# The decode tile and the first full tile of an input projection share each weight block: five products a block, x in halves, wide dummy products

## The chip, the cores and the metric

One core of a Trainium2 chip runs the whole layer in one launch. The metric is the device time of a run in microseconds (us); less is better. The kernel before took 2188.03 us (median of 3 runs, 2186.51 to 2188.49). TensorE (PE) multiplies matrices; VectorE (DVE), ScalarE (ACT) and GpSimd (POOL) work on elements; SyncE (SP) here only starts DMA transfers. ACT and POOL start some too.

## The reference

The layer steps 2048 frames of a new stream and 64 frames of a running one (the decode frames), each of 1024 values. What the change touches is its first line, the projection of the normed frames by one weight with 2816 columns:

```python
def _project(a, w_in, pos):
    z = a @ w_in                                   # a: frames x 1024, w_in: 1024 x 2816
    qa, ka, va, qr, kr, vr, gr = jnp.split(z, SPLITS, axis=-1)
    ...                                            # rotate qa, ka, qr, kr by position

a = _rmsnorm(hp, norm1[l])                         # hp: 2048 prompt frames
qa, ka, va, qr, kr, vr, gr = _project(a, w_in[l], pos_p)
attn_o = _swa_prompt(qa, ka, va, sinks[l])
ret_o, s_p = _retention_prompt(qr, kr, vr)
hp = hp + _mix_out(attn_o, ret_o, gr, w_out[l])
hp = hp + _sqrelu_mlp(_rmsnorm(hp, norm2[l]), w_up[l], w_down[l])
...                                                # the same for hs, the 64 decode frames
```

`_attend` is attention over a window with sinks, `_retention_chunk` a recurrent attention by chunks with a state. Everything is fp32, the keys, values and states are outputs as well, and the last norm ends the layer.

## The kernel before

**Tiles.** The frames form 17 tiles: 16 full ones of 128 prompt frames, and the decode tile of 64 frames, here S (its index in the code is `S`, 16). The columns of the weight are worked in two phases of 1408 (`ph`), each in three column groups `ci` of 384, 512 and 512 columns: group 0 has the attention's query, key and value, groups 1 and 2 the retention's. The first unit of phase 0 is the pair (S, tile 0). Tile 0 is the first full tile, T below; the tile after it is the third tile. The unit goes through the groups in the order S group 0, T group 0, S group 1, T group 1, S group 2, T group 2; the units after it have one tile each.

**Products.** An fp32 value is kept as a high part and a low part, and a product of two values is made of three: high times high, high times low, low times high. The 1024 rows of a weight group lie in 8 blocks `k` of 128 rows. For a full tile each block takes three products: xh with wh (L599), xh with wl (L600), xl with wh (L602). The decode tile has only 64 frames, so its high and low parts lie side by side in one operand xh of 128 columns, and two products do (L599, L600); then the two halves of the result are added (`zb` L607, `zz` L608). The result z of a group is gathered in one PSUM bank.

**Loads and splits.** A weight block comes by SP's queue (`load_w`, L117) into a raw buffer, and `split_scaled` makes wh on ACT (L85) and wl on DVE (L86), scaled by the norm's gain `gsb`. The raw blocks of group 0 and 1 have eight buffers between them. The transposed x of a tile comes by `load_x` (L140) or, for the first two tiles, in two halves of four blocks (`load_part`, L640). `split_x` makes xh on ACT (L151) and xl on DVE for the first two tiles (L153), on POOL in four pieces for all later ones (L156). xh and xl have two buffers each, so the third tile's xh goes into S's buffer, once S's last product is done. For a full tile, the halves and the whole x are read from `xt`, where the 128 values of one row, block and tile (512 bytes) lie together.

**Order.** At the program's start ACT issues S's first half of x, the gains and S's second half; SP issues the eight blocks of group 0 (0-weights: a "c-weight" is a block of group c), then T's two halves, then the 1-weights, S's rows of x for the norm (`xk`, by `load_aux`), the 2-weights with the cache `cf` (L482, L483), the states. ACT and DVE split S's x, the eight 0-weights, then T's x. Eighteen dummy products (`idle`, L634) go first on PE. PE and SP follow the order in which the code is written. ACT, DVE and POOL are ordered by a scheduler.

**Small stages.** Between the products of the groups a planner sets the short stages of attention and retention of each tile (att_a to att_e, ret_a to ret_e). `run_ready` is asked before each block; it goes by a modelled clock that each block's products move on, by latencies `LAT` and by costs `COST`, and sets a stage when its inputs are due. So a change in the order of the products changes where the stages of the tiles behind it stand. Names of the stages' instructions that come up: `zr` and `qk` are rotated by three instructions on DVE and one addition on POOL (L215); pq (L267 to L271) and ptr (L415) are transposes on PE; rqT (L425) and rkT (L423) are copies of ptr that pss (L431), a product of the retention stage, waits for. `token_norm` (L176 to L179) and `token_rest` (L187 to L189) make the norm's factors; nsk (L667) holds the negated sinks.

Of the kernel before, what the change touches and what calls it, by code (L numbers as in the profile page):

```python
# [11 lines left out]
F32 = mybir.dt.float32  # L12
F32R = mybir.dt.float32r
AF = mybir.ActivationFunctionType
# [25 lines left out]
def body(ctx, tc, xt, xd, xtok, w1, wout, wup, wdn, gains, sinks, ck, cv, sret, rot, rdec, qdec, dmask,  # L40
# [93 lines left out]
    def load_x(t, first=False, tag="xr"):  # L134
        t0, T = tok(t)
        xr = xp.tile([128, NK, 128], F32, name="xr", tag=tag, bufs=1)
        if T < 128:
            xr = xr.rearrange("p k t -> p (k t)")[:, :NK * T].rearrange("p (k t) -> p k t", k=NK)
        if not first:
            nc.sync.dma_start(xr, xt[:, :, t0:t0 + T] if T == 128 else xd)  # L140
        return xr

    def split_x(t, xr, first=False):

        t0, T = tok(t)
        xh = xp.tile([128, NK, 128], F32R, name="xh")
        xl = xp.tile([128, NK, 128], F32R, name="xl") if T == 128 else None
        for a in (slice(0, 4), slice(4, 8)) if first else (slice(0, 8),):
            h = xh[:, a, :T]
            l = xl[:, a, :] if T == 128 else xh[:, a, 64:128]  # L150
            nc.scalar.activation(h, xr[:, a, :T], AF.Copy)  # L151
            if first:
                nc.vector.tensor_sub(l, xr[:, a, :T], h.bitcast(F32))  # L153
            else:
                for k in range(0, NK, 2):
                    nc.gpsimd.tensor_sub(l[:, k:k + 2], xr[:, k:k + 2, :T], h[:, k:k + 2].bitcast(F32))  # L156
        return xh, xl
# [12 lines left out]
    last_act, last_dve = [None], [None]  # L170
# [415 lines left out]
    def group(ph, t, ci, n_):  # L586
# [7 lines left out]
        z = psum("z") if (n_, ci) == (1, 2) else zp.tile([128, 512], F32, name="z")  # L594
        for k in range(NK):
            run_ready(clock[0])
            s = ws[ph, ci][k]
            wh, wl = s[:, 0], s[:, 1]
            nc.tensor.matmul(z[:, :n], xh[:, k], wh, start=k == 0, stop=False)  # L599
            nc.tensor.matmul(z[:, :n], xh[:, k], wl, start=False, stop=k == NK - 1 and xl is None)  # L600
            if xl is not None:
                nc.tensor.matmul(z[:, :n], xl[:, k], wh, start=False, stop=k == NK - 1)  # L602
            clock[0] += (2 if xl is None else 3) * n * 0.4237e-3
# [13 lines left out]
        if (n_, ci) == (0, 1):  # L617
            do_stage("att_a", *tiles[1])
            done["z0", 1] = clock[0]

    slow = {0: 2.4, 1: 2.4, **dict.fromkeys((2, 4, 15, 16, 17, 18, 20, 32), 2.0)}
# [11 lines left out]
    for _ in range(18):  # L633
        nc.tensor.matmul(idle[:, 0:128], idr, ones, start=True, stop=True)  # L634
    a, b = tiles[:2]
    xraw = {0: load_x(a[1], True)}

    def load_part(n, k):
        t0, T = tok(tiles[n][1])
        (nc.sync if n else nc.scalar).dma_start(xraw[n][:, k:k + 4, :T], xt[:, k:k + 4, t0:t0 + T] if T == 128 else xd[:, k:k + 4])  # L640

    load_part(0, 0)
    nc.scalar.dma_start(gsb, gains)
    load_part(0, 4)
    first = cp.tile([128, 3], F32, name="first")
    nc.scalar.activation(first, mhalf, AF.Copy)
    raws = [load_w(0, 0, k, True) for k in range(NK)]
    x0 = split_x(a[1], xraw[0], True)
    ws[0, 0] = weights(0, 0, raws)
    xraw[1] = load_x(b[1], True, "xk")  # L650
    for k in range(2):
        load_part(1, 4 * k)
    x1 = split_x(b[1], xraw[1], True)
# [10 lines left out]
    raws.append(load_w(0, 2, NK - 1))  # L664
    load_states(0)
# [588 lines left out]
def _arrays(x_prompt, x_sample, cache_k, cache_v, state_ret, norm1, w_in, sinks, w_out, norm2, w_up, w_down, norm_f):  # L1254
# [22 lines left out]
    return dict(xt=xt, xd=f(xt[:, :, SEQ:]), xtok=f(xa), w1=w1, wout=wout, wup=wup, wdn=wdn,  # L1277
# [23 lines left out]
```

## Time and profile before

| | before |
|---|---|
| runs, median (3) | 2188.03 us (2186.51 to 2188.49) |
| the profiled execution's own time | 2188.54 us |
| its span in the profile | 2186.8 us |
| granted TensorE clock, mean over the span | 0.998 |
| PE busy | 2169.5 us, 99% of the span |
| weight loads of PE (PEld) busy | 2085.7 us, 95% |
| DVE, ACT, POOL busy | 70%, 52%, 20% |
| moved by DMA | 515.92 MB, 236 GB/s |

The profile is of one execution, whose own time is 1.74 us longer than its span; times in its rows count from the span's start. A row of the timeline gives the start of an instruction, its duration, engine, line and operation, output <- inputs, the shape, and in brackets how long the engine had waited and for what. Of a matmul the duration overlaps the next one's start, so the pace is read from one start to the next. A row of the groups has the busy time and the mean duration in ns, then the idle time ahead of the group and what ended most of it. A row of the DMA issues has the number of transfers, the size of one and the median time from issue to landing.

### The profile page before, as it was taken

How to read it: one execution, taken by the hardware profiler on the slowest of the kernel's cores; microseconds unless marked ns; L12 is line 12 of the kernel's file. 1: busy time of each engine (PE TensorE's matmuls, PEld its weight loads, DVE VectorE, ACT ScalarE, POOL GpSimd, SP SyncE). 2: the span in 40 equal slices, each digit the busy share in tenths (PEclk: the TensorE clock that was granted, in tenths of full speed). 3: DMA queues.
4: the chain of work that ended last, by engine and by line, in shares of the span. 5: the costliest groups of instructions: out<-in, count | busy, mean ns of one | idle time of the engine just before them, and what ended most of it. 6: DMA issues, size and time to landing. Idle time of an engine off the chain costs nothing.

```text
span 2186.8 us, 35871 instructions
## 1 busy us (share of the span) xinstructions
PE 2169.5 (99%) x13170; PEld 2085.7 (95%) x13170; DVE 1519.9 (70%) x2698; ACT 1139.6 (52%) x2114; POOL 439.5 (20%) x577
## 2 busy tenths in 40 slices
PE   9999999999999999999999999999999999999998
PEld 7888888889888999999999999999999999999998
DVE  6576668566666685887787677667666876687665
ACT  6455555544445533555665566556545544554452
POOL 4545554444433222000000000000001200120011
PEclk9999999999999999999999999999999999999999
DMA  6667964788544897699799678666977777777662
GB/s 193 182 180 197 246 180 132 198 220 214 136 118 144 314 328 243 218 313 313 254 350 323 229 265 293 235 231 218 375 251 240 275 269 239 245 277 272 231 214 82
DMA packets 242927, 515.92 MB, mean 236 GB/s; under 512 B 21168, under 2 KB 128368, under 8 KB 238656
## 3 DMA queue, kind: packets, MB, share of 16 engines
q1 hardware_dynamic: 232224, 469.35, 63.3%
q0 software_dynamic: 8512, 43.29, 9.3%
q8 instruction: 103, 1.69, 0.3%
q10 hardware_dynamic: 2016, 1.00, 0.2%
q14 instruction: 72, 0.59, 0.1%
HBM read 411.19 MB, written 169.54 MB: 266 GB/s over the span
## 4 chain that ended last, share of the span: by engine, by line
PE 90%; DVE 1%; DMA 1%; ACT 1%; issue 0%; POOL 0%; SPq 0%; DVEq 0%; ACTq 0%
PE y L1165 10%; PE y L1164 10%; PE y L1163 10%; PE z L599 6%; PE z L600 6%; PE z L602 6%; PE b L999 4%; PE b L998 4%; PE b L997 4%; PE y L857 3%; PE y L859 3%; PE y L858 3%; PE a L999 3%; PE a L998 3%; PE a L997 3%; PE c L999 3%
## 5 line engine op out<-in xcount | busy, mean ns | idle before, releaser
L1165 PE MATMUL y<-vh,wd 128*128 128x352 f32 x1344 | 434.0, 323 | 0.8 <-DVE wd L534 0.8
L1164 PE MATMUL y<-vl,wd 128*128 128x352 f32 x1344 | 433.5, 323 | 0.0
L1163 PE MATMUL y<-vh,wd 128*128 128x352 f32 x1344 | 431.4, 321 | 0.0
L599 PE MATMUL z<-w,xh 128*128 128x512 f32 (+1 forms) x816 | 320.3, 392 | 0.1
L1115 POOL TENSOR_TENSOR acc<-acc,sq 128x352 f32<-128x352 f32 x41 | 71.1, 1735 | 1213.3 <-ACT sq L1114 1213.3
L600 PE MATMUL z<-w,xh 128*128 128x512 f32 (+1 forms) x816 | 305.7, 375 | 1.2 <-DVE w L86 1.1
L533 ACT ACTIVATE wd<-dr 128x1024 fp32r<-128x1024 f32 x168 | 177.4, 1057 | 246.5 <-PE y L1165 175.3
L533 ACT ACTIVATE wu<-upr 128x512 fp32r<-128x512 f32 x336 | 209.3, 627 | 177.7 <-PE b L999 88.2
L602 PE MATMUL z<-w,xl 128*128 128x512 f32 (+1 forms) x768 | 287.0, 374 | 0.1
L534 DVE TENSOR_TENSOR wu<-upr,wu 128x512 fp32r<-128x512 f32 x336 | 230.5, 692 | 72.1 <-ACT wu L533 57.9
L534 DVE TENSOR_TENSOR wd<-dr,wd 128x1024 fp32r<-128x1024 f32 x168 | 209.0, 1246 | 97.3 <-ACT wd L533 96.6
L1165 PEld LDWEIGHTS y<-vh,wd 128*128 128x128 f32 x1344 | 252.7, 188 | 1.1 <-DVE wd L534 1.1
L1164 PEld LDWEIGHTS y<-vl,wd 128*128 128x128 f32 x1344 | 252.4, 188 | 0.0
L1163 PEld LDWEIGHTS y<-vh,wd 128*128 128x128 f32 x1344 | 252.3, 188 | 0.0
L998 PE MATMUL b<-al,wu 128*128 128x352 f32 x576 | 185.8, 323 | 0.0
L999 PE MATMUL b<-ah,wu 128*128 128x352 f32 x576 | 185.5, 323 | 0.0
L997 PE MATMUL b<-ah,wu 128*128 128x352 f32 x576 | 184.9, 321 | 0.0
L600 PEld LDWEIGHTS z<-w,xh 128*128 128x128 f32 x816 | 154.9, 190 | 19.8 <-DVE w L86 3.5
L599 PEld LDWEIGHTS z<-w,xh 128*128 128x128 f32 x816 | 154.8, 190 | 16.9 <-ACT w L85 0.4
L534 DVE TENSOR_TENSOR vl<-rv,vh 128x1408 fp32r<-128x1408 f32 x84 | 137.6, 1640 | 43.4 <-ACT vh L533 42.9
L602 PEld LDWEIGHTS z<-w,xl 128*128 128x128 f32 x768 | 144.1, 188 | 21.6 <-DVE xl L153 0.4
L533 ACT ACTIVATE vh<-rv 128x1408 fp32r<-128x1408 f32 x84 | 116.0, 1381 | 63.9 <-DMA rv<-vscr 46.4
(291 smaller groups left out, 4777.4 us busy)
## 6 DMA issues: line engine op xcount, KB each, us to landing
rv<-vscr SPq DMA_DIRECT2D x84, 704.0 KB, 5.4
vscr<-C SPq DMA_DIRECT2D x48, 1056.0 KB, 5.7
upr<-uscr SPq DMA_DIRECT2D x192, 256.0 KB, 5.1
dr<-sscr SPq DMA_DIRECT2D x96, 512.0 KB, 4.7
upr<-in_wup SPq DMA_DIRECT2D x144, 256.0 KB, 3.8
dr<-in_wdn SPq DMA_DIRECT2D x72, 512.0 KB, 5.4
uscr<-in_wup POOLq DMA_DIRECT2D x16, 1024.0 KB, 10.0
sscr<-in_wdn POOLq DMA_DIRECT2D x16, 1024.0 KB, 9.0
```

What stands on the lines that cost most here:

```text
L533: nc.scalar.activation(h, x, AF.Copy)
L534: return nc.vector.tensor_sub(l, x, h.bitcast(F32))
L599: nc.tensor.matmul(z[:, :n], xh[:, k], wh, start=k == 0, stop=False)
L600: nc.tensor.matmul(z[:, :n], xh[:, k], wl, start=False, stop=k == NK - 1 and xl is None)
L602: nc.tensor.matmul(z[:, :n], xl[:, k], wh, start=False, stop=k == NK - 1)
L997: nc.tensor.matmul(o, wh, ah[:, k], start=k == 0 and i in (1, 6, 5), stop=False, skip_group_check=True)
L998: nc.tensor.matmul(o, wh, al[:, k], start=False, stop=False, skip_group_check=True)
L999: nc.tensor.matmul(o, wl, ah[:, k], start=False, stop=k == 3 and i in (2, 4, 3), skip_group_check=True)
L1115: nc.gpsimd.tensor_add(self.acc, self.acc, sq)
L1163: nc.tensor.matmul(o, wh, vh, start=f == 0, stop=False)
L1164: nc.tensor.matmul(o, wh, vl, start=False, stop=False)
L1165: nc.tensor.matmul(o, wl, vh, start=False, stop=f == 15)
```

## The change

The first unit, S and T, is made in another way in phase 0; all else stays.

1. **Products.** For each block S's two products are followed by T's three. In group 0 T lags two blocks behind S. `group` makes the products of both when it is called for S; when it is called for T, it takes the z that is there. T's z of groups 1 and 2 is in the pool `pp`, that of group 0 in `zp`.
2. **x in halves.** A new input `xq` holds each full tile's x on its own, so that half a tile's row lies together (2048 bytes instead of four pieces of 512). T's first half is issued by ACT, its second by SP between the fifth and the sixth 0-weight. ACT's queue now issues the gains, S's first half, T's first half, S's second half. ACT and DVE split in this order: S's first half, 0-weights 0 and 1, T's first half, 0-weights 2 and 3, S's second half, 0-weight 4, T's second half, 0-weights 5 to 7.
3. **Dummies.** Nine of 512 columns in place of eighteen of 128.
4. **Third tile.** Its x is issued on SP right behind the last 2-weight, ahead of the states. T's attention stage att_a is bound to be issued behind the newest split of x on ACT.

```diff
 def load_x(t, first=False, tag="xr"):
-            nc.sync.dma_start(xr, xt[:, :, t0:t0 + T] if T == 128 else xd)
+            nc.sync.dma_start(xr, xq[t] if T == 128 else xd)
...
 def split_x(t, xr, first=False):
-        for a in (slice(0, 4), slice(4, 8)) if first else (slice(0, 8),):
+        def part(a):
...
-            nc.scalar.activation(h, xr[:, a, :T], AF.Copy)
+            last_xh[0] = nc.scalar.activation(h, xr[:, a, :T], AF.Copy)
...
+        if first:
+            return (xh, xl), part
+        part(slice(0, 8))
         return xh, xl
...
 def group(ph, t, ci, n_):
-        z = psum("z") if (n_, ci) == (1, 2) else zp.tile([128, 512], F32, name="z")
-        for k in range(NK):
-            run_ready(clock[0])
...
+        def products(z, x, k):
+            h, l = x
+            wh, wl = ws[ph, ci][k][:, 0], ws[ph, ci][k][:, 1]
+            nc.tensor.matmul(z[:, :n], h[:, k], wh, start=k == 0, stop=False)
+            nc.tensor.matmul(z[:, :n], h[:, k], wl, start=False, stop=k == NK - 1 and l is None)
+            if l is not None:
+                nc.tensor.matmul(z[:, :n], l[:, k], wh, start=False, stop=k == NK - 1)
+            clock[0] += (2 if l is None else 3) * n * 0.4237e-3
+
+        if n_ != 1:
+            z = zp.tile([128, 512], F32, name="z")
+            pair = [(z, xs[ph, t][:2], 0)]
+            if n_ == 0:
+                other[ci] = psum("z") if ci else zp.tile([128, 512], F32, name="z")
+                pair.append((other[ci], xs[tiles[1]][:2], 0 if ci else 2))
+            for k in range(NK + pair[-1][2]):
+                run_ready(clock[0])
+                for y, x, lag in pair:
+                    if 0 <= k - lag < NK:
+                        products(y, x, k - lag)
+        else:
+            z = other[ci]
...
         if (n_, ci) == (0, 1):
-            do_stage("att_a", *tiles[1])
+            with tc.issue_after(last_xh[0].ins):
+                do_stage("att_a", *tiles[1])
...
-    for _ in range(18):
-        nc.tensor.matmul(idle[:, 0:128], idr, ones, start=True, stop=True)
+    for _ in range(9):
+        nc.tensor.matmul(idle, idr, ones.unsqueeze(1).broadcast_to([128, 4, 128]), start=True, stop=True)
...
-    load_part(0, 0)
     nc.scalar.dma_start(gsb, gains)
-    load_part(0, 4)
+    load_part(nc.scalar, 0, 0)
+    load_part(nc.scalar, 1, 0)
+    load_part(nc.scalar, 0, 4)
...
-    raws = [load_w(0, 0, k, True) for k in range(NK)]
-    x0 = split_x(a[1], xraw[0], True)
-    ws[0, 0] = weights(0, 0, raws)
...
+    raws = [load_w(0, 0, k, True) for k in range(5)]
+    load_part(nc.sync, 1, 4)
+    raws += [load_w(0, 0, k, True) for k in range(5, NK)]
...
+    lo, hi = slice(0, 4), slice(4, 8)
+    for f, y, ks in ((part0, lo, (0, 1)), (part1, lo, (2, 3)), (part0, hi, (4,)), (part1, hi, (5, 6, 7))):
+        f(y)
+        ws[0, 0] += weights(0, 0, raws, ks)
...
     raws.append(load_w(0, 2, NK - 1))
+    xraw[2] = load_x(tiles[2][1])
     load_states(0)
```

PE's order at the start of the program, before the change: the dummies, then S's products of group 0 (z_293 is S's result, xh_149 its x, w1_0_0_k the 0-weight k). T's follow behind the sixteenth.

```order
L634 MATMUL idle_108<-ones_73,idr_71 128x128 x18
L599 MATMUL z_293<-w1_0_0_0_154,xh_149 128x384
L600 MATMUL z_293<-w1_0_0_0_154,xh_149 128x384
L599 MATMUL z_293<-w1_0_0_1_157,xh_149 128x384
L600 MATMUL z_293<-w1_0_0_1_157,xh_149 128x384
L599 MATMUL z_293<-w1_0_0_2_160,xh_149 128x384
L600 MATMUL z_293<-w1_0_0_2_160,xh_149 128x384
```

The same place now; z_286 and xh_143 are S's, z_287, xh_144 and xl_145 are T's, and the lines are those of the changed code.

```order
L652 MATMUL idle_108<-ones_73,idr_71 128x512 x9
L601 MATMUL z_286<-w1_0_0_0_148,xh_143 128x384
L602 MATMUL z_286<-w1_0_0_0_148,xh_143 128x384
L601 MATMUL z_286<-w1_0_0_1_151,xh_143 128x384
L602 MATMUL z_286<-w1_0_0_1_151,xh_143 128x384
L601 MATMUL z_286<-w1_0_0_2_156,xh_143 128x384
L602 MATMUL z_286<-w1_0_0_2_156,xh_143 128x384
L601 MATMUL z_287<-w1_0_0_0_148,xh_144 128x384
L602 MATMUL z_287<-w1_0_0_0_148,xh_144 128x384
L604 MATMUL z_287<-w1_0_0_0_148,xl_145 128x384
L601 MATMUL z_286<-w1_0_0_3_159,xh_143 128x384
```

T's first products stand behind six of S, so T's xh and xl are needed after the third block; before, they were needed after the eighth.

PE's order at S's last product (xh_149), before the change: it stands at the end of S's part of group 2, and T's 24 products of that group follow (z_509, xh_181, xl_182), with small stages between them.

```order
L599 MATMUL z_464<-w1_0_2_7_290,xh_149 128x512
L600 MATMUL z_464<-w1_0_2_7_290,xh_149 128x512
L599 MATMUL z_509<-w1_0_2_0_269,xh_181 128x512
L600 MATMUL z_509<-w1_0_2_0_269,xh_181 128x512
L602 MATMUL z_509<-w1_0_2_0_269,xl_182 128x512
```

The same place now: xh_361 and xl_362 are the third tile's, and xh_361 has the buffer of xh_143.

```order
L601 MATMUL z_455<-w1_0_2_7_283,xh_143 128x512
L602 MATMUL z_455<-w1_0_2_7_283,xh_143 128x512
L601 MATMUL z_456<-w1_0_2_7_283,xh_144 128x512
L602 MATMUL z_456<-w1_0_2_7_283,xh_144 128x512
L604 MATMUL z_456<-w1_0_2_7_283,xl_145 128x512
L601 MATMUL z_542<-w1_0_0_0_148,xh_361 128x384
L602 MATMUL z_542<-w1_0_0_0_148,xh_361 128x384
L604 MATMUL z_542<-w1_0_0_0_148,xl_362 128x384
```

Three products lie between S's last one and the third tile's first one, where 24 and some stages lay.

POOL's order at the third tile's low half, before: xl_346 in four pieces stands behind qk_402 of S, the two loads of the cache for the other phase (cf_8111), and zr_411 with three small instructions of T.

```order
L667 TENSOR_SCALAR nsk_77<-sk_76 128x8
L215 TENSOR_TENSOR qk_402<-rot1_403,rot2_404 64x512
L482 DMA cf_8111<-in_cv 128x64
L483 DMA cf_8111<-in_ck 128x64
L215 TENSOR_TENSOR zr_411<-rot1_413,rot2_414 128x320
L187 TENSOR_SCALAR hrs_82<-rs_81 128x1
L188 TENSOR_SCALAR ss_80<-ms_258 128x1
L189 TENSOR_SCALAR rsv_83<-rd_105,rs_81 128x4
L156 TENSOR_TENSOR xl_346<-xr_343,xh_345 128x256 x4
```

POOL's order there now; xl_362 is the third tile's low half, qk_418 is S's.

```order
L218 TENSOR_TENSOR qk_418<-rot1_419,rot2_420 64x512
L690 TENSOR_SCALAR nsk_77<-sk_76 128x8
L485 DMA cf_8102<-in_cv 128x64
L486 DMA cf_8102<-in_ck 128x64
L156 TENSOR_TENSOR xl_362<-xr_254,xh_361 128x256 x4
L218 TENSOR_TENSOR zr_427<-rot1_429,rot2_430 128x320
```

zr of T has gone behind the low half; qk, nsk and the two DMA issues are still ahead of it. From here to about the 1484th row on PE the stages of later tiles stand elsewhere than before; behind that the orders are equal.

More of the change, by code (lines that the diff above doesn't have):

```diff
@@ L39, in body @@
 @with_exitstack
-def body(ctx, tc, xt, xd, xtok, w1, wout, wup, wdn, gains, sinks, ck, cv, sret, rot, rdec, qdec, dmask,
+def body(ctx, tc, xt, xq, xd, xtok, w1, wout, wup, wdn, gains, sinks, ck, cv, sret, rot, rdec, qdec, dmask,
          yT, nkp, nvp, nrp, nks, nvs, nrs):
@@ L169, in body @@
     squares = {}
-    last_act, last_dve = [None], [None]
+    last_act, last_dve, last_xh = [None], [None], [None]
     def token_norm(t):
@@ L593, in group @@
         n = CN[ci]
-        z = psum("z") if (n_, ci) == (1, 2) else zp.tile([128, 512], F32, name="z")
-        for k in range(NK):
-            run_ready(clock[0])
[L597 to L603, printed above, removed]
+        def products(z, x, k):
[19 more added lines that the diff above has]
+            z = other[ci]
         if xl is None:
@@ L617, in group @@
         if (n_, ci) == (0, 1):
-            do_stage("att_a", *tiles[1])
+            with tc.issue_after(last_xh[0].ins):
+                do_stage("att_a", *tiles[1])
             done["z0", 1] = clock[0]
+    other = {}
     slow = {0: 2.4, 1: 2.4, **dict.fromkeys((2, 4, 15, 16, 17, 18, 20, 32), 2.0)}
@@ L632, in body, with load_part @@
     idle = psum("idle")
-    for _ in range(18):
-        nc.tensor.matmul(idle[:, 0:128], idr, ones, start=True, stop=True)
+    for _ in range(9):
+        nc.tensor.matmul(idle, idr, ones.unsqueeze(1).broadcast_to([128, 4, 128]), start=True, stop=True)
     a, b = tiles[:2]
[L636 to L640, printed above, removed]
-    load_part(0, 0)
+    xraw = {0: load_x(a[1], True), 1: load_x(b[1], True, "xk")}
+    def load_part(eng, n, k):
+        t = tiles[n][1]
+        eng.dma_start(xraw[n][:, k:k + 4], xq[t, :, k:k + 4] if t < S else xd[:, k:k + 4])
     nc.scalar.dma_start(gsb, gains)
-    load_part(0, 4)
+    load_part(nc.scalar, 0, 0)
+    load_part(nc.scalar, 1, 0)
+    load_part(nc.scalar, 0, 4)
     first = cp.tile([128, 3], F32, name="first")
     nc.scalar.activation(first, mhalf, AF.Copy)
-    raws = [load_w(0, 0, k, True) for k in range(NK)]
-    x0 = split_x(a[1], xraw[0], True)
-    ws[0, 0] = weights(0, 0, raws)
[L650 to L653, printed above, removed]
+    raws = [load_w(0, 0, k, True) for k in range(5)]
+    load_part(nc.sync, 1, 4)
+    raws += [load_w(0, 0, k, True) for k in range(5, NK)]
+    x0, part0 = split_x(a[1], xraw[0], True)
+    x1, part1 = split_x(b[1], xraw[1], True)
+    ws[0, 0] = []
+    lo, hi = slice(0, 4), slice(4, 8)
+    for f, y, ks in ((part0, lo, (0, 1)), (part1, lo, (2, 3)), (part0, hi, (4,)), (part1, hi, (5, 6, 7))):
+        f(y)
+        ws[0, 0] += weights(0, 0, raws, ks)
     raws = [load_w(0, 1, k, True) for k in range(NK)]
@@ L1276, in _arrays @@
     rd, qd, dm = _decay_tables()
-    return dict(xt=xt, xd=f(xt[:, :, SEQ:]), xtok=f(xa), w1=w1, wout=wout, wup=wup, wdn=wdn,
+    xq = f(xt[:, :, :SEQ].reshape(128, 8, SEQ // 128, 128).transpose(2, 0, 1, 3))
+    return dict(xt=xt, xq=xq, xd=f(xt[:, :, SEQ:]), xtok=f(xa), w1=w1, wout=wout, wup=wup, wdn=wdn,
                 gains=gains, sinks=sk, ck=f(np.asarray(cache_k)[0, 0]), cv=f(np.asarray(cache_v)[0, 0]),
```

## The prediction

> **What bounds the kernel now.** I read the page first, for the engine that is nearly never idle.
>
> ```profile
> PE 2169.5 (99%) x13170; PEld 2085.7 (95%) x13170; DVE 1519.9 (70%) x2698; ACT 1139.6 (52%) x2114; POOL 439.5 (20%) x577
> ```
>
> TensorE (PE) is busy for 99% of the span, and the change leaves its products as many as they were. So time can only come from places where PE waits or runs slowly, and what is saved at the start moves everything behind it forward. I therefore read PE's timeline of the first 40 us, from start to start: a busy matmul overlaps its successor, so the distance between starts tells more than the duration. First the 18 dummies, then the first products of the decode tile (S; the first full tile is T below, and a block of column group c is a "c-weight"):
>
> ```profile
> 1.75 4.10 PE L634 MATMUL idle<-ones,idr 128*128 128x128 f32 x18 [1.75 <-DVE ones L61]
> 5.65 0.63 PE L599 MATMUL z<-w,xh 128*128 128x384 f32 x1
> 6.08 0.52 PE L600 MATMUL z<-w,xh 128*128 128x384 f32 x1
> 6.40 0.52 PE L599 MATMUL z<-w,xh 128*128 128x384 f32 x1
> ...
> 9.56 0.34 PE L599 MATMUL z<-w,xh 128*128 128x384 f32 x1
> ```
>
> A 384-wide product takes 0.32 us here (6.08 to 6.40), and the rows go on like that until 9.56. Later it takes 0.17 (14.95 to 15.12), and a 512-wide one 0.23 (15.12 to 15.35):
>
> ```profile
> 14.95 0.34 PE L602 MATMUL z<-w,xl 128*128 128x384 f32 x1
> 15.12 0.39 PE L599 MATMUL z<-w,xh 128*128 128x512 f32 x1
> 15.35 0.40 PE L600 MATMUL z<-w,xh 128*128 128x512 f32 x1
> ...
> 26.05 0.24 PE L267 MATMUL pq<-idf,zr 64*64 64x64 f32 x1
> ...
> 26.72 0.50 PE L599 MATMUL z<-w,xh 128*128 128x512 f32 x1
> ```
>
> From 5.65 to 26.05 PE does groups 0 and 1 of both tiles: 40 x 0.173 + 40 x 0.228 = 16.04 us of work in 20.40, so 4.36 are lost to the slow pace and to waits for T's x and for 1-weights. Group 2 has two holes, and the third tile one:
>
> ```profile
> 29.67 0.40 PE L599 MATMUL z<-w,xh 128*128 128x512 f32 x1
> 30.39 0.50 PE L600 MATMUL z<-w,xh 128*128 128x512 f32 x1 [0.32 <-DVE w L86]
> 30.73 0.40 PE L599 MATMUL z<-w,xh 128*128 128x512 f32 x1
> 31.32 0.50 PE L600 MATMUL z<-w,xh 128*128 128x512 f32 x1 [0.20 <-DVE w L86]
> ...
> 38.55 0.34 PE L602 MATMUL z<-w,xl 128*128 128x384 f32 x1
> 39.79 0.39 PE L431 MATMUL pss<-rqT,rkT 128*64 128x64 f32 x3 [0.90 <-ACT rkT L423]
> ```
>
> 0.72 - 0.23 = 0.49, 0.59 - 0.23 = 0.36, and 0.11 each for the slower product after them: 1.07. pss waits 1.24 - 0.17 = 1.07. **Lost before: 6.5 us.**
>
> **The change: loads and splits at the start.** ScalarE's (ACT's) second and third issue, and what landed how long after its issue:
>
> ```profile
> 1.15 0.45 ACTq L643 DMA_DIRECT2D gsb<-in_gains  x1
> 1.63 0.45 ACTq L640 DMA_DIRECT2D xr<-in_xd  x1
> ```
>
> ```profile
> wraw<-in_w SPq DMA_DIRECT2D x8, 192.0 KB, 3.6
> xr<-in_xt SPq DMA_DIRECT2D x2, 256.0 KB, 5.4
> xr<-in_xd ACTq DMA_DIRECT2D x2, 128.0 KB, 3.2
> gsb<-in_gains ACTq DMA_DIRECT2D x1, 12.0 KB, 2.9
> ```
>
> The work on a block and on half an x, on ACT and then on VectorE (DVE):
>
> ```profile
> L85 ACT ACTIVATE w<-wraw,gsb 128x384 fp32r<-128x384 f32 x8 | 4.5, 605 | 0.8 <-DMA wraw<-in_w 0.7
> ...
> L151 ACT ACTIVATE xh<-xr 128x512 fp32r<-128x512 f32 x2 | 1.3, 632 | 1.2 <-DMA xr<-in_xt 1.1
> ```
>
> ```profile
> L86 DVE SCALAR_TENSOR_TENSOR w<-wraw,gsb,w 128x384 fp32r<-128x384 f32 x8 | 4.6, 615 | 0.9 <-ACT w L85 0.9
> L153 DVE TENSOR_TENSOR xl<-xr,xh 128x512 fp32r<-128x512 f32 x2 | 1.4, 692 | 1.2 <-ACT xh L151 1.2
> L153 DVE TENSOR_TENSOR xh<-xr,xh 128x256 fp32r<-128x256 f32 x2 | 0.8, 422 | 2.4 <-ACT xh L151 2.4
> ```
>
> Gains go first now, so S's first half is issued second, at 1.15, and lands near 4.1. ACT splits it to 4.5 and 0-weights 0 and 1 to 5.7. T's first half is issued third, at 1.63. In the old layout such a half took 5.4 to land; in the new one it lies like the weights, which took 3.6. I take 4.0, nearer to the weights it resembles (ends 3.6 and 5.4): landed 5.6, at the latest 7.0. ACT splits it 5.7 to 6.3, DVE 6.3 to 7.0, and then the low part of weight 2 by 7.6. Up to there PE has five products to do. 35 remain: 35 x 0.173 = 6.06. DVE's blocks (0.62, with 0.42 and 0.69 for the two other halves) stay just ahead of PE's five products (0.87); I allow 0.3 for holes. Group 0 ends at 13.95: 13.95 - 5.65 - 6.92 = **1.4 lost** (1.1 without holes, 2.8 if the half lands at 7.0).
>
> SP issues T's second half between the fifth and the sixth block. ACT began the last block at 9.01:
>
> ```profile
> 9.01 0.61 ACT L85 ACTIVATE w<-wraw,gsb 128x384 fp32r<-128x384 f32 x1 [0.23 <-DMA wraw<-in_w]
> ```
>
> Split by 9.01 + 0.61 + 0.62 = 10.2; PE now comes to it ten products before 13.95, at 12.2. This slack of 2.0 hides the 256 KB ahead of it; without it each microsecond would count fully.
>
> **The wide dummies.** Nine of 512 columns at the slow pace take 9 x 0.32 x 512/384 = 3.84 us, against 4.10: PE is free near 5.6 either way. Before, the pace rose 3.9 us after dense products began (5.65 to 9.56). If wide dummies are as dense, it rises at 1.75 + 3.9 = 5.65 and no real product is slow. If they are not, those from 7.6 to 9.56 are: 1.96 x (1 - 0.173/0.32) = 0.9. I take 0.
>
> [...]
>
> **Groups 1 and 2.** A block now gives PE 5 x 0.228 = 1.14 us of work and costs DVE about 0.75:
>
> ```profile
> 21.89 0.75 DVE L86 SCALAR_TENSOR_TENSOR w<-raw,gsb,w 128x512 fp32r<-128x512 f32 x1 [1.81 <-ACT w L85]
> ...
> 30.53 0.73 DVE L86 SCALAR_TENSOR_TENSOR w<-raw,gsb,w 128x512 fp32r<-128x512 f32 x1
> ```
>
> So the waits in group 1 go; it runs from 13.95 to 23.1. The first 2-weight was ready at 22.6, in time; the next follow the rotation of S and come about as wanted: 0.1 (0 to 0.5). The last was ready at 31.3; PE comes to its low part at 23.1 + 7 x 1.14 + 0.67 (pq, 26.05 to 26.72) + 0.23 = 32.0. Group 2 ends at 32.9.
>
> **What is late next: the third tile's x.** Its high half goes into S's buffer. S's last product stood 24 products before the end of group 2; now it stands four before it. ACT's row, and GpSimd's (POOL's), which makes the low half:
>
> ```profile
> 31.90 1.06 ACT L151 ACTIVATE xh<-xr 128x1024 fp32r<-128x1024 f32 x1 [0.56 <-PE z L600]
> ```
>
> ```profile
> 30.11 0.61 POOL L667 TENSOR_SCALAR nsk<-sk 128x8 f32<-128x8 f32 x1
> 30.68 1.87 POOL L215 TENSOR_TENSOR qk<-rot,rot 64x512 f32<-64x512 f32 x1
> 32.51 0.63 POOL L482 DMA_DIRECT2D cf<-in_cv  x1
> ...
> 35.40 2.81 POOL L156 TENSOR_TENSOR xl<-xr,xh 128x256 fp32r<-128x256 f32 x4
> 38.18 1.27 POOL L215 TENSOR_TENSOR qk<-rot,rot 128x512 f32<-128x512 f32 x1
> ```
>
> ACT began 0.58 after S's last product (31.32 to 31.90). Now that is 32.9 - 4 x 0.23 + 0.58 = 32.6, done 33.65: PE waits 0.85. POOL has qk, nsk and two DMA issues ahead of the low half. DVE does the same work as before by 31.3, the last weight behind the rotations, so qk starts near 30.6 and POOL is free at 30.6 + 1.87 + 0.61 + 2 x 0.6 = 34.3; the first quarter is there at 35.0. PE wants it two products after 32.9, at 33.25: **1.75 lost**, the 0.85 within it. The other quarters take 0.70 each and PE six products, 1.04, so they wait no more. Ends: 1.2 if POOL is free when ACT is done, 2.5 if DVE's rotations come 0.75 later.
>
> By the 128x512 row qk takes 1.27, and the wait is 1.2. [...]
>
> pss stands after two blocks of the third tile's group 1 now, near 41, and I reckon ACT's rkT at 40: its 1.07 goes.
>
> **Sum.** 6.5 - (1.4 + 0.1 + 1.75) = 3.25 gained. The profiled execution took 2188.54, 0.51 above the runs' median of 2188.03: 2185.3 for one like it, by the median **2184.8**. About 0.2%, 4.4 us, is what a measurement of this kernel can tell from no change: below 2183.6 is faster.
>
> **Rivals.** *All covers hold*: POOL is free in time (1.2), group 0 has no holes (1.1), group 2 none, and the new order loses one later wait (0.5 to 0.8). 6.5 - 2.3 + 0.7 = 4.9: 2183.1. For it: 1.87 is a single slow instance. Against: it takes three things at once.
>
> *The new order of the small stages*: the planner moves the stages of some 15 tiles, up to about 290 us. Waits of that kind exist; pss has two more, near 340 and 353:
>
> ```profile
> PE pss L431 <- DVE rqT L425: 2.7, 2, 1.8
> ```
>
> One or two new ones of 0.9 to 1.8 leave a gain of about 1: 2187.0.
>
> *The clock stays down*, the slower side: PE's holes before 7.6 and behind it keep it from being busy enough. With all 35 products at 0.32, group 0 ends at 18.8 instead of 13.95: 4.85 more, 2189.7. It decides once the slow pace lasts past 7.6 + 3.25 x 0.32/0.147 = 14.7. Against it: the pace rose after 3.9 dense us, and dense work now stands from 1.75. [...]
>
> **Chances.** Forecast 0.62: 2183.8 (1.1 and 1.2 for the two waits) to 2186.2 (the half at 7.0). All covers hold 0.13, new order 0.18, clock 0.07. Faster by over 0.2%: 0.13, and 0.04 of the forecast, whose edge lies closer to the bound than the runs spread (2186.51 to 2188.49): 0.17. Slower by over 0.2%: 0.03, the ends of the last two. Within: 0.80. The range, 2182.8 to 2187.2, holds the forecast, the first rival and most of the second.
>
> **What would show it.** Right: products 0.17 apart from about 7.6 on, group 0 done near 14, no hole in group 1, group 2 done near 33, then waits at the third tile's first products for ACT's xh and POOL's xl, 1.75 together. Wrong: slow products after 9; ACT idle for T's first half beyond 6; holes over 0.5 in group 1; a wait at the third tile under 1 or over 2.5; new waits of PE between 60 and 300 us.

## The result and the profile after

The changed kernel took 2200.53 us (median of 6 runs, 2197.89 to 2202.15), the kernel before 2187.27 in the runs beside it (6 runs, 2185.25 to 2190.7). The ratio is 1.006, with an interval of 1.0049 to 1.007: 13.3 us slower, where 2184.8 was forecast and a range of 2182.8 to 2187.2. The profiled execution took 2202.15 us with a span of 2200.4, so 13.6 more than that of before.

First PE's timeline at the start, at the rows that the prediction spoke of.

```profile
1.75 4.21 PE L652 MATMUL idle<-ones,idr 128*128 128x512 f32 x9 [1.75 <-DVE ones L61]
6.16 0.66 PE L601 MATMUL z<-w,xh 128*128 128x384 f32 x1 [0.20 <-ACT w L85]
...
7.25 0.34 PE L601 MATMUL z<-w,xh 128*128 128x384 f32 x1
...
8.69 0.45 PE L602 MATMUL z<-w,xh 128*128 128x384 f32 x1 [0.31 <-DVE w L86]
...
14.87 0.39 PE L601 MATMUL z<-w,xh 128*128 128x512 f32 x1
...
33.72 0.39 PE L604 MATMUL z<-w,xl 128*128 128x512 f32 x1
34.58 0.45 PE L601 MATMUL z<-w,xh 128*128 128x384 f32 x1 [0.47 <-ACT xh L151]
...
35.60 0.44 PE L604 MATMUL z<-w,xl 128*128 128x384 f32 x1 [0.39 <-POOL xl L156]
```

The start is what was forecast, about 1 us late. Group 0 ends at 14.87 instead of 13.95; groups 1 and 2 take 19.08 us up to 33.95 (33.72 and one product of 0.23) instead of 18.95; then the third tile's x comes late by 0.63 (33.95 to 34.58) and by some 0.6 (35.60). The third tile's first product stands at 34.58, against 38.20 before.

The loss is behind that. The waits of PE over the whole span, longest first (in total, how many, the longest):

```profile
PE z L601 <- DVE sig L412: 6.1, 2, 3.1
PE pss L434 <- DVE rqT L428: 2.3, 2, 1.8
PE idle L652 <- DVE ones L61: 1.7, 1, 1.7
PE y L880 <- ACT wo L536: 1.6, 2, 0.9
...
PE z L601 <- DVE rot L217: 1.0, 1, 1.0
```

The first row is new: twice PE stood for 3.07 us ahead of a group's first product. All engines around the first of these places, rows of the chain that PE waited for:

```profile
69.28 0.61 PE L449 MATMUL pst<-vs,qk 128*128 128x128 f32 x4
69.48 0.28 ACT L454 ACTIVATE ro<-pr 128x128 f32<-128x128 f32 x1 [0.96 <-PE pr L444]
...
70.57 0.73 POOL L456 TENSOR_TENSOR rr<-s,mhalf 128x2 f32<-128x2 f32 x1
71.34 0.61 DVE L470 SCALAR_TENSOR_TENSOR ro<-pr,rr,sig 128x128 f32<-128x128 f32 x2 [0.92 <-POOL rr L456]
71.98 0.47 ACT L410 ACTIVATE sig<-z,hrs 128x256 f32<-128x256 f32 x1 [1.36 <-DVE ro L470]
...
72.49 0.42 DVE L412 SCALAR_TENSOR_TENSOR sig<-sig,z 128x256 f32<-128x256 f32 x1 [0.54 <-ACT sig L410]
...
72.96 0.79 PE L601 MATMUL z<-w,xh 128*128 128x512 f32 x1 [3.07 <-DVE sig L412]
```

pr and pst are ret_d of T. Its last step, ro, reads the one buffer of sig; only then ret_v of the third tile can write sig, and only when that is done is the bank free which holds the third tile's z of group 2. There are three banks for z, so the fourth tile's group 2 wants just this bank. In the order of before, T's ret_d stood ahead of the last block of the fourth tile's group 0, nine blocks earlier. Now it stands behind the last block of that tile's group 1, directly ahead of the product that waits for it. The second hole, at 94.7 us, is the same one tile later.

The clock fell behind the holes. Windows of 2 us of PE: its busy time, its instructions, the granted clock, the DMA share and GB/s.

```profile
70.00:72.00 2.00, 0.00 (x0) 1.00 0.00 0
72.00:74.00 2.00, 1.04 (x3) 0.52 0.00 0
74.00:76.00 2.00, 2.00 (x8) 0.50 0.71 230
76.00:78.00 2.00, 2.00 (x6) 0.50 0.92 278
78.00:80.00 2.00, 2.00 (x8) 0.77 0.95 363
80.00:82.00 2.00, 2.00 (x12) 1.00 0.65 264
```

In windows of 0.2 us the clock is 0.50 from 72.1 to 78.9 and from 99.4 to 102.8. PE worked at half speed for 5.9 us (from 72.96) and for 3.4: 3.0 and 1.7 lost.

The sum: pst is usually followed after 0.36 us, here after 3.68, so 3.32 for each hole; with the clock 6.64 + 4.7 = 11.3. The wait for rot ahead of the fourth tile's group 0 adds 1.15 with the slower product behind it; it has the same root, since the third tile's norm stands on ACT behind T's sig, which waits for S's ro. Against this stand the 2.7 that the start had gained by the fourth tile (55.22 without that wait, against 58.85, less an estimated 0.95 of stages that stand later now). That makes 9.8 of 13.6. Of the rest, 1.9 are two waits for the output weights near 709 and 740 us (the row wo, with the slower product behind each). Another 1.7 is a half clock from 365.6 to 369.0 us, behind the wait of 1.81 for pss that the kernel before has as well, there with no dip behind it. Together 13.4.

### The profile page after: what moved, and what is told of

Its sections match the earlier page's. It is cut to its first block, busy times and chain, and to the rows that moved or that the text cites. A ratio compares the mean times of both kernels' runs of the same rounds, so it can differ in the third digit from the quotient of the medians.

```text
span 2200.4 us, 35874 instructions
## 1 busy us (share of the span) xinstructions
PE 2175.5 (99%) x13161; PEld 2088.2 (95%) x13161; DVE 1523.5 (69%) x2698; ACT 1140.3 (52%) x2114; POOL 442.3 (20%) x577
## 3 DMA queue, kind: packets, MB, share of 16 engines
q10 hardware_dynamic: 2160, 1.26, 0.2%
## 4 chain that ended last, share of the span: by engine, by line
PE 93%; DMA 2%; DVE 2%; ACT 1%; POOL 1%; issue 1%; SPq 0%; ACTq 0%; DVEq 0%; POOLq 0%
PE y L1188 10%; PE y L1187 10%; PE y L1186 9%; PE z L601 7%; PE z L602 7%; PE z L604 7%; PE b L1022 4%; PE b L1021 4%; PE b L1020 4%; PE a L1022 3%; PE a L1021 3%; PE c L1022 3%; PE a L1020 3%; PE c L1021 3%; PE c L1020 3%; PE y L880 3%
## 6 DMA issues: line engine op xcount, KB each, us to landing
uscr<-in_wup POOLq DMA_DIRECT2D x16, 1024.0 KB, 10.2
```

## The experiments

Theory **late stage**, later **order**: the loss is the new order of the small stages on PE. Rival **dense start**: the pairing itself brings the clock down later. Then the question was what the change is worth without the order.

**The latencies of S.** S's group 1 is finished one group of T later when it is paired, so S's retention stages come later, and T's wait for S's buffers. The planner stretches S's latencies by a number:

```diff
-    slow = {0: 2.4, 1: 2.4, **dict.fromkeys((2, 4, 15, 16, 17, 18, 20, 32), 2.0)}
+    slow = {0: 2.0, 1: 2.4, **dict.fromkeys((2, 4, 15, 16, 17, 18, 20, 32), 2.0)}
```

> The changed kernel with one number of the planner changed: the stretch of the latencies of S's stages from 2.4 to 2.0. T's and the third tile's ret_d then stand in the order where they stood before the change (T's six blocks into the fourth tile's group 0, in place of the end of its group 1). Theory late stage (ret_d stands right ahead of a group 2 whose z bank is only freed by work behind ret_d; the clock drops in these holes): both waits of 3.07 us for sig go, the granted clock stays 1.00 between 60 and 110 us, and the time is 2200.5 - 2 x 3.3 - 2.95 - 1.7 - 1.1 = 2188 or up to 4 less, 2184 to 2188. Rival dense start (the pairing's denser start and moved loads bring the clock down later, wherever the stages stand): the dips stay, 2197 to 2201.

2191.57 us (11 runs), ratio 1.0016 (1.0007 to 1.0024): 9 of the 13.3 us came back, but not all. The waits for sig and their dips are gone; another hole, with a clock of 0.50 behind it from 112.8 to 116.2 us, has come in the sixth tile's group 1:

```profile
112.13 0.46 PE L444 MATMUL pr<-vs,sd 128*128 128x128 f32 x2 [3.35 <-DVE sd L437]
```

**Another bank.** The order stays, but the waiting group gets a bank of the small stages' pool.

```diff
-            z = zp.tile([128, 512], F32, name="z")
+            z = psum("z") if (n_, ci) in ((3, 2), (4, 2)) else zp.tile([128, 512], F32, name="z")
```

> The changed kernel with the order on TensorE untouched, but the z of group 2 of the fourth and fifth tile taken from the pool of the small stages' banks, so that it needn't wait for the z of the tile before. Theory late stage: the two holes at 70 and 94.5 us shrink below 1 us, no dip of the clock, 2200.5 - 11.3 = 2189 (2187 to 2191). If ret_d's place stops TensorE by another buffer than z's bank, a wait of some 3 us stands at another line, 2197 to 2201. Rival dense start: the dips stay, 2197 to 2201.

2195.41 us (5 runs), 1.0034 (1.0021 to 1.0047). Both waits for sig went. pst of T is followed after 0.36 (70.28 to 70.64), and PE keeps its pace behind it, 512-wide products 0.23 apart from 73.15 to 75.64, where the changed kernel's clock was 0.50; so the bank was what PE waited for, and this dip came with its hole. The time missed the 2187 to 2191, since other waits took their place, the largest one for POOL:

```profile
101.09 0.66 PE L418 MATMUL ptr<-idf,qk 128*128 128x128 f32 x4 [2.03 <-POOL qk L218]
```

**The cause put into the kernel before.**

```diff
-        return None if any(x is None for x in ts) else max(ts)
+        return None if any(x is None for x in ts) else max(ts) + (4.0 if name == "ret_d" and n in (1, 2) else 0.0)
```

> The kernel before, with 4 us added to the due time that the planner gives ret_d of T and of the third tile, nothing else. T's ret_d moves into the fourth tile's group 1 (four blocks ahead of its group 2), the third tile's to the end of the fifth tile's group 1, right ahead of its group 2. Theory late stage: one hole of about 3.3 us at the fifth tile's group 2 with a clock of 0.5 behind it for 3.4 to 6 us (1.7 to 3 us lost), and under 1 us for T's: 2187.3 + 5 to 6.5, 2192 to 2194. Rival dense start: without the paired start no dip, 2187 to 2189.

2190.66 us (11 runs, 2188.0 to 2193.6), 1.0016 (1.0007 to 1.0025), less than the 2192 to 2194 expected. The profiled run, 2193.17, has the hole and a dip of 6.8 us; here the row of the waits and one window:

```profile
PE z L599 <- DVE sig L409: 3.4, 2, 3.1
```

```profile
96.00:100.00 4.00, 4.00 (x12) 0.50 0.94 288
```

So hole and dip come without any pairing. That the runs lie as much as 5.6 us apart fits a dip that some runs have and others not. Every run's mean granted clock is on record: 0.996 or 0.997 in five of the six runs above 2190 us, 0.998 in all five below.

**Group 0 alone paired.**

```diff
-        if n_ != 1:
-            z = zp.tile([128, 512], F32, name="z")
+        if (n_, ci) != (1, 0):
+            z = psum("z") if (n_, ci) == (1, 2) else zp.tile([128, 512], F32, name="z")
...
-            if n_ == 0:
+            if (n_, ci) == (0, 0):
```

> The changed kernel with only group 0 paired; groups 1 and 2 go S first and then T, as before. S's z of group 1 is then done one group of T (5.4 us) sooner, and ret_d of T stands seven blocks and that of the third tile eight blocks ahead of the group 2 behind them. Theory late stage: no hole of 3 us, no dip; the start keeps what group 0 brings (about 1 to 2 us), group 1's waits for weights come back in part: 2184 to 2188. Rival dense start (group 0's dense products and dummies): 2197 to 2201.

2195.77 us (6 runs), 1.0035 (1.0022 to 1.0047): a miss. The holes for sig are not there, but the planner's list for this kernel has others, each with a clock of 0.50 behind it (from 123.9 us on, and from 185.3 to 188.7):

```profile
122.67 0.71 PE L434 MATMUL pss<-rqT,rkT 128*128 128x128 f32 x4 [2.15 <-ACT rkT L426]
```

```profile
184.73 1.06 PE L349 MATMUL pt<-idf,p 128*128 128x128 f32 x4 [3.17 <-DVE p L335]
```

Each of these kernels has an order of its own, with holes of its own. To part the order from the rest, the next two take the planner out and set the stages from a list, by tile number, group and block.

**The changed kernel with the order of before.** The list of before from the fourth tile on, ahead of it a few places set by hand:

```diff
+    PLAN = {}
+    for w in """
+    0.2.4:att_b0 2.0.2:ret_b0 2.0.7:att_c0 2.1.1:ret_c0 2.1.2:att_b1 2.1.4:ret_b1 2.1.6:ret_d0 2.2.2:ret_c1
...
+    """.split():
+        at, what = w.split(":")
+        PLAN[at] = [(x[:5], int(x[5:])) for x in what.split(",")]
...
-    def run_ready(limit):
+    def run_ready(*at):
+        for name, n in PLAN.pop(".".join(map(str, at)), ()):
+            st = next(q for q in queue if q[:2] == (name, n))
+            queue.remove(st)
+            do_stage(name, st[2], st[3])
```

> The changed kernel with the planner taken out: the small stages are set from a written list. From the fourth tile's group 0 on it is the list of the kernel before; S's and T's stages until then are set by hand within the third tile's groups. All else (pairs, halves, dummies, loads) is as changed. Theory order (the whole loss is the new order of the small stages, each bad place a hole of some 3 us with a slower clock behind it, and the change itself brings the 3.4 us that the start shows): no wait of TensorE over 2.1 us before 340 us, clock 1.00 there, 2187.5 - 3.4 = 2184, 2182 to 2186. Rival another cost (banks, loads or engines behind the pairs cost time whichever order): 2189 or more, as in the run with the shorter latency.

2187.63 us (11 runs) beside 2187.52: 1.0003 (0.9994 to 1.0012). All of the loss is gone, but nothing is gained either, so the time misses the 2182 to 2186. Its profiled run (2189.49) shows where the start's gain went in that run. PE's rows, its windows of 1 us, and its waits:

```profile
8.72 0.44 PE L635 MATMUL z<-w,xh 128*128 128x384 f32 x1 [0.98 <-ACT w L85]
9.47 0.45 PE L636 MATMUL z<-w,xh 128*128 128x384 f32 x1 [0.31 <-DVE w L86]
```

```profile
10.00:11.00 1.00, 1.00 (x5) 0.58 0.96 314
11.00:12.00 1.00, 1.00 (x5) 0.50 0.81 281
12.00:13.00 1.00, 1.00 (x5) 0.50 0.89 270
13.00:14.00 1.00, 1.00 (x6) 0.71 0.97 344
```

```profile
PE pr L444 <- DVE sd L437: 1.4, 1, 1.4
```

Here the pace rose near 7 us (a 384-wide product took 0.66 at 6.17 and 0.34 at 7.05) and the clock fell to 0.50 from 10.2 to 13.6, behind the holes at 7.3 to 9.5: group 0 ended at 17.2, not at 14.9. Of the nine profiles with wide dummies and a paired group 0, three have this second dip (this one, from 9.3 to 12.7 the one with the fills below, from 9.5 to 13.0 the one with group 0 alone and the order of before) and six have not; the ends of group 0 lie between 14.4 and 17.2. A wait of 1.39 for sd, up to 111.09 us, and one of 0.7 for the output weights take more.

**The kernel before with the new order.** The same machine, with the list that the planner made for the changed kernel; nothing else of the change.

> The kernel before, with the small stages set from the list that the planner made for the changed kernel; nothing else of the change. Theory order: the two holes of 3.07 us ahead of group 2 of the fourth and the fifth tile stand here too, 1.1 us at the fourth tile's group 0, and behind each hole a clock of 0.5 in most runs (0 to 4.7 us in all): 2187.5 + 7 to 12, 2195 to 2200. Rival another cost: the order alone takes less than half of the 13 us, below 2194.

2198.16 us (5 runs), 1.005 (1.0037 to 1.0062): 10.6 of the 13.3 us without a pair, a half or a wide dummy. Its waits and windows:

```profile
PE z L633 <- DVE sig L409: 6.2, 2, 3.1
```

```profile
72.00:76.00 4.00, 1.45 (x4) 0.74 0.00 0
76.00:80.00 4.00, 4.00 (x17) 0.83 0.95 263
```

These two settle it: the order of the stages, with what the scheduler makes of it on ACT, DVE and POOL, moves the time by about the whole loss in both directions.

**Narrow dummies.** The kernel with the written list, with eighteen dummies of 128 columns.

```diff
-    for _ in range(9):
-        nc.tensor.matmul(idle, idr, ones.unsqueeze(1).broadcast_to([128, 4, 128]), start=True, stop=True)
+    for _ in range(18):
+        nc.tensor.matmul(idle[:, 0:128], idr, ones, start=True, stop=True)
```

> The changed kernel with the written list, but eighteen dummies of 128 columns instead of nine of 512. Theory of the dummies (the wide ones bring the fast pace near 7 us instead of 9.6): slow products until 9.6 or later, less what TensorE would wait for weights and x anyway: 0.5 to 1.5 us slower than with the wide ones. Rival: the pace rises when it likes and the first weights bound the start: no difference over 0.4 us.

2188.61 us (11 runs), 1.0007 (0.9998 to 1.0016). The median is 1.0 above that with the wide ones, but the intervals overlap: not decided. What the dummies do to the pace is clearer. In this profile 384-wide products are 0.32 apart from 10.22 on, with three or four of them in each half microsecond up to 14.5 us and five in the next. In the kernel before, with narrow dummies too, the fast pace comes at 9.56. With wide ones a 384-wide product first takes 0.34 to 0.36, after 0.66, at 7.25 in the changed kernel, at 7.05 with the written list and at 6.88 with the stages moved below.

**The holes filled.** Twelve dummies ahead of the two groups that wait.

```diff
+                if (n_, ci, k) in ((3, 2, 0), (4, 2, 0)):
+                    fill = psum("fill")
+                    for _ in range(12):
+                        nc.tensor.matmul(fill, idr, ones.unsqueeze(1).broadcast_to([128, 4, 128]), start=True, stop=True)
```

> The changed kernel with twelve dummy products of 512 columns (2.7 us) ahead of group 2 of the fourth and of the fifth tile, where TensorE waits 3.07 us. If the clock drops because TensorE is idle there: the clock stays 1.00, the holes stay about as long but filled, and the time is 2200.5 less the 4.65 us of half clock that the profile shows, or less where runs have no drop: 2196 to 2199. If the clock drops for another reason: dips as before, 2199 to 2202.

2197.32 us (5 runs), 1.0043 (1.003 to 1.0055): 3.2 below the changed kernel, as expected if the clock falls because PE is idle. The size is not secure: the two kernels were not run side by side, and their intervals (1.003 to 1.0055 and 1.0049 to 1.007) overlap. PE's rows at the first place and the windows that hold the two fills:

```profile
71.51 3.01 PE L618 MATMUL fill<-ones,idr 128*128 128x512 f32 x12
74.83 0.50 PE L601 MATMUL z<-w,xh 128*128 128x512 f32 x1 [0.32 <-DVE sig L412]
```

```profile
72.00:76.00 4.00, 3.69 (x18) 1.00 0.00 0
...
96.00:100.00 4.00, 3.69 (x21) 1.00 0.41 118
```

The chain is as long as before (pst at 71.14, the product at 74.83), and the clock is 1.00 in every window from 68 to 108 us, where it was 0.50 behind the unfilled holes. So it is the idleness in the holes that brings these dips.

**Group 0 alone, order of before.** The edit of the fourth run, and the list of before as a whole.

> The changed kernel with only group 0 paired (as in the run above with group 0 alone) and the small stages set from the list of the kernel before, whole. Theory order: the two places of 2.3 and 3.3 us that the planner's list had at 120 and 181 us with half clock behind one of them go, 2195.8 - 8 = 2187.5 or less; with a start that is 1.5 to 2.5 us better than before's and the 0.9 us at 697 us that all kernels with the new loads show, 2185.5 to 2187.5. If pairing costs time whichever list: 2190 or more.

2190.89 us (11 runs) beside 2188.61, 1.0012 (1.0003 to 1.002). The holes of its planner's list are gone, 4.9 us came back, but the gain of the start is not seen either, and the time lies in the range named for "pairing costs time whichever list". Pairing as such need not cost time, since the changed kernel with the written list pairs all three groups and loses nothing. In the profile here the clock dips from 9.5 to 13.0 and from 354.3 to 357.7, and DVE splits a 2-weight late; how much of the 2.3 us is due to these stays open:

```profile
31.99 0.50 PE L636 MATMUL z<-w,xh 128*128 128x512 f32 x1 [1.16 <-DVE w L86]
```

**The old layout of x.** The written list, but x from the array `xt`.

```diff
-            nc.sync.dma_start(xr, xq[t] if T == 128 else xd)
+            nc.sync.dma_start(xr, xt[:, :, t0:t0 + T] if T == 128 else xd)
...
-        eng.dma_start(xraw[n][:, k:k + 4], xq[t, :, k:k + 4] if t < S else xd[:, k:k + 4])
+        eng.dma_start(xraw[n][:, k:k + 4], xt[:, k:k + 4, 128 * t:128 * t + 128] if t < S else xd[:, k:k + 4])
```

> The changed kernel with the written list, but each x read from the old array (512-byte pieces), and the new input left out. If the new layout brings T's first half sooner: ACT's split of it starts 1 us later or more than 7.5 us, and 0.5 to 1.5 us are lost, 2188 to 2189.5. If the layout does nothing for the start (halves landed 5.1 to 5.9 us after their issue, as against 5.4 before): 2187 to 2188. If the new input is behind the wait of 0.7 to 1.9 us for the output weights near 700 us, that wait goes here; else it stays.

2189.41 us (11 runs) beside 2188.61, 1.0007 (0.9998 to 1.0016): no difference from the new layout's 1.0003 that the intervals could show. ACT's split of T's first half, first in this kernel:

```profile
7.30 0.63 ACT L151 ACTIVATE xh<-xr 128x512 fp32r<-128x512 f32 x1 [1.11 <-DMA xr<-in_xt]
```

and in the changed kernel:

```profile
6.75 0.63 ACT L151 ACTIVATE xh<-xr 128x512 fp32r<-128x512 f32 x1 [0.18 <-DMA xr<-in_xq]
```

In the kernel with the written list and the new layout it started at 7.54. With the new layout this half landed 5.1 us after its issue in the changed kernel, 5.0 with the shorter latency, 5.9 with the written list and 4.6 with the stages moved below, here after 5.6. The wait for the output weights stayed (0.7), so the new input isn't behind it. The profiled run, 2186.74 and the fastest of the eleven, has no second dip at the start and shows the start's gain: the fourth tile's group 0 begins at 56.50 us, against 58.85 in the kernel before and 58.32 in the profiled run of the written list, which has the dip.

**Wide dummies alone**, in the kernel before (the edit of the narrow dummies, turned round).

> The kernel before with the nine wide dummies alone; the order of all else is as before. If the fast pace comes near 7 us instead of 9.6: S's products of group 0 then wait for the splits of the weights (0.62 us a block on VectorE against 0.64 at the slow pace), so 0 to 0.6 us gained, 2187.0 to 2187.5. If denser dummies brought the whole gain of the start: 2185.5 or less.

2192.42 us (11 runs) beside 2188.61, 1.002 (1.0011 to 1.0029): 3.8 slower, a miss. PE's order is that of before, but the scheduler that orders ACT, DVE and POOL had other lengths to reckon with and put other work ahead of the last 2-weights. PE, and then DVE:

```profile
29.76 0.51 PE L600 MATMUL z<-w,xh 128*128 128x512 f32 x1 [1.07 <-DVE w L86]
...
32.28 0.58 PE L600 MATMUL z<-w,xh 128*128 128x512 f32 x1 [1.78 <-DVE w L86]
```

```profile
29.91 1.03 DVE L231 TENSOR_TENSOR kw<-pq,kw 64x128 fp32r<-64x128 f32 x4
30.86 0.58 DVE L286 TENSOR_TENSOR qT<-pq,qT 64x128 fp32r<-64x128 f32 x2
31.48 0.75 DVE L86 SCALAR_TENSOR_TENSOR w<-raw,gsb,w 128x512 fp32r<-128x512 f32 x1
```

Before, this last split began at 30.53, ahead of kw; now kw and qT stand ahead of it. Behind the second wait 512-wide products start 0.43 us apart (32.66 to 33.94); from 27.13 to 27.59 it was 0.23.

**Three stages moved by hand** in the written list:

```diff
-    4.0.0:ret_e1,att_d1 4.0.6:ret_d2 4.1.0:att_c2 4.1.1:ret_c3
+    4.0.0:ret_e1,att_d1 4.1.0:att_c2 4.1.1:ret_d2,ret_c3
...
-    16.2.2:ret_c15
...
-    18.0.0:ret_c16
+    16.2.4:ret_c15 18.0.4:ret_c16
```

> The changed kernel with the written list, in which three stages are set later, each behind a wait that the profile of the run with that list shows: ret_d of the fifth tile by three blocks (its pr waited 1.35 us for sd), and ret_c of two tiles near 341 and 354 us by two and by four blocks (their pss waited 0.76 and 1.81 us for rqT, as in the kernel before). Theory order: the three waits go and no others come, 2187.6 - 1.4 - 0.9 - 2.0 = 2183.3, 2182.5 to 2185.5, faster than both kernels. Rival (each move has the compiler order the other engines anew, and new waits come for old ones): 2186.5 or more.

2192.11 us (11 runs) beside 2188.09, 1.0018 (1.0009 to 1.0027): the time is the rival's. But the first of the three moves was not the one meant. The wait for sd stood in the sixth tile's group 1, where the list sets the fifth tile's ret_d (5.1.5):

```profile
111.09 0.46 PE L444 MATMUL pr<-vs,sd 128*128 128x128 f32 x2 [1.39 <-DVE sd L437]
```

The edit moved the third tile's ret_d (4.0.6), which stood at 81.50 us and had not waited. All three old waits are gone all the same, this one too, with its stage where it was. New waits came, the longest right behind the ret_d that was moved, with a half clock from 85.4 to 88.8 behind it:

```profile
85.14 1.01 PE L434 MATMUL pss<-rqT,rkT 128*128 128x128 f32 x4 [1.88 <-ACT rkT L426]
```

```profile
346.68 0.46 PE L444 MATMUL pr<-vs,sd 128*128 128x128 f32 x2 [1.30 <-DVE sd L437]
```

So new waits came for old ones, as the rival said; what the two moves of ret_c are worth without the wrong one was not run.

No kernel of this study is shown to be faster than the one before.

## Why the prediction was wrong

**The start came nearly as forecast.** 3.25 us were to be gained up to pss; the profile shows 2.7 by the fourth tile. Group 1 lost nothing, group 2 about 0.1, pss near 42 us no longer waits, the third tile's x cost 1.2, the lower end given, since POOL's qk took 1.27 and not 1.87. The 1.87 was one row of the kernel before, where qk began at 30.68, while DVE made its last split (30.53 to 31.26). Here that split ended at 30.49 and qk began at 32.15. That the one made the other longer was not shown.

**Two terms of it were mis-sized.** T's first half was to land at 5.6, by the weights' 3.6 us; it landed near 6.7, as slowly as in the old layout. The pace was to rise 3.9 us after dense work began, at 5.65; it rose at 7.2, 5.5 us after the first dummy. That the 3.9 us of the kernel before would hold for wide dummies was an estimate, and no run shows it. The rival that the clock stays down was in the right place: in three of nine profiles it fell again near 10 us, which costs half of 3.4 us.

**The step that failed** is the cost of *the new order of the small stages*. The forecast's sum has no term for it. As a rival it was named, at a chance of 0.18, but priced by single waits for pss in the trace of before: "One or two new ones of 0.9 to 1.8 leave a gain of about 1: 2187.0." What came were two waits of 3.07 and one of 1.0, and a half clock behind the long ones: 12.5 us in place of 0.9 to 3.6. The price was not to be read from a wait in the old profile, since the old order was free of this one. It follows from the chain behind ret_d, whose durations are all in rows like those of the first hole: two squares on ACT, two steps on POOL, two on DVE, sig on ACT and on DVE. And the place could be seen in the two orders: the prediction compared them at the start and at the third tile only, and took the rest, some 250 us, as one lump. The nine blocks by which T's ret_d moved stood there. The prediction's own sign of this, new waits between 60 and 300 us, came at 69.9 and 94.7. The forecast's 0.62 also rested on the sum of the start as if nothing behind it could answer; the slower side had 0.03.

**The clock behind a hole** was in no term. The run with the fills puts it at about 3 us for two holes, the profile at 4.7, and it also fell behind a wait that both kernels have.

What stays open: why every kernel built on the changed one waits 0.7 us or more for the output weights near 700 us, while of the kernel before and the three built on it one waits 0.3 and the others not at all; and how often the start's second dip comes, since each kernel was profiled once.

## What to carry to other kernels

Where a planner or a scheduler sets the order in which the engines work, a change of a few microseconds at the start is a change of the whole order: compare both orders to the place where they agree again, and for each stage that came nearer to a buffer's next use, add up the chain that frees the buffer. To tell an edit's worth from the order's, run the new code with the old order and the old code with the new one. Where a wait can't be removed, dummy products in it are worth a run: the twelve here kept the clock at 1.00 in two waits behind which it had been 0.50.

## What the runs showed of the hardware

The dips given here with both ends last about 3.41 us or twice that. The clock reads 0.50 from 72.09 to 78.91, from 99.39 to 102.81 and from 365.63 to 369.05 in the changed kernel, from 74.0 to 77.4 and 97.9 to 101.3 in the kernel before with the new order, from 93.5 to 100.3 in the one with the cause put in. From 7.23 us, where the changed kernel's record starts, to the fall at the program's end (2191.76), the stretches between two changes are 64.85, 6.83, 20.48, 3.41, 262.83, 3.41 and 1822.72 us: 19, 2, 6, 1, 77, 1 and 534 times 3.413. In the kernel before there is one stretch, from 9.48 to the fall at 2176.95, 635 times as long.

PE need not have been idle all the time ahead of a dip: the 3.41 us before the one at 99.39 hold 1.81 of waiting and 1.60 of products. And a wait of the same length had a dip behind it in one profile and none in another. Thirteen of the fourteen profiles have the wait of 1.8 for pss between 350 and 366 us. In five of them a clock of 0.50 follows for 3.4 us (the changed kernel, the other bank, the cause put in, the fills, group 0 alone with the order of before); in the other eight the clock reads 1.00 from 346 to 376 us (one is the kernel before's). First the changed kernel's row, then the one of the kernel before:

```profile
365.51 1.13 PE L434 MATMUL pss<-rqT,rkT 128*128 128x128 f32 x4 [1.81 <-DVE rqT L428]
```

```profile
355.14 0.71 PE L431 MATMUL pss<-rqT,rkT 128*128 128x128 f32 x4 [1.81 <-DVE rqT L425]
```

These two differ in where the wait lies in the steps of 3.41 us, counted back from the fall at the end. In the changed kernel the wait, 363.70 to 365.51, lies whole in the step from 362.22 to 365.63, and the dip begins where the step ends. In the kernel before the wait, 353.33 to 355.14, is parted at 354.23 into 0.90 and 0.91. From 14 us to the end, the steps of the changed kernel with most waiting hold 2.19 (68.67 to 72.09), 1.81 (95.98 to 99.39) and 1.81 (362.22 to 365.63), and its three dips begin behind these; behind the next, with 1.26 (92.57 to 95.98), none does. But the fall at the end comes behind 1.10 there and behind 0.93 in the kernel before, so these two traces give no amount of waiting that brings a fall. The start gives none either: from 7.0 to 9.5 us PE is idle for 1.29, 1.29 and 1.45 us in the three profiles with the second dip, and for 1.70 in that of the other bank, which has none.

The dips of 6.8 us have the wait still going on when they begin, for 0.87 us in the changed kernel and 0.73 in the one with the cause put in; in the dip of 3.41 at 74.0, with the new order, it went on for 0.59.

So what was measured is that behind holes of 1.8 to 3.4 us the clock was at 0.50 for 3.41 or 6.83 us in some profiles, and behind a hole of 1.8 in others not. That the place of a wait among the steps decides is the author's estimate from the two traces. With one profile of each kernel, no run shows what it does to the scatter between runs.

At the start the recorded clock doesn't help: the windows read 1.00 from 5 us on in the narrow-dummy run too, whose products are 0.32 apart until 14 us. There the pace has to be read from the starts of the products.

A POOL addition (zr of S, 64x320) took 4.90 us at 23.39 in the changed kernel, where its twin took 1.32 at 23.77 in the kernel before. DVE split weights beside both (23.24 to 27.28 and 23.61 to 25.63), so what made the one longer was not shown. It was hidden here.
